# Two empty tiles of 32 bytes around the pool of the normalised activations

## Chip, core and metric

The kernel runs on one core of a Trainium2 chip. The metric is device time in microseconds (us) for one execution. The kernel before takes 1226.62 us, the median of three runs that lie between 1225.09 and 1227.04 us.

## What is computed

One decoder layer of a hybrid model on a sequence of 256 tokens, model width 2048, all in float32. The reference, cut to its frame:

```python
h = rms_norm(x, attn_norm_g[l])
proj = h @ w_in[l]                       # 2048 -> 4448 columns
shifted = token_shift(proj[..., :RWKV_SHIFT_DIM], rwkv_mu[l])
...
y_rwkv = rwkv7_mixer(h_r, h_k, h_v, h_w, h_a, h_g, ...)   # 16 heads x 64, a recurrence over tokens
y_mla = mla_mixer(c_q, c_kv, k_pe, positions, ...)        # 8 heads, causal attention
y = jnp.concatenate([y_rwkv, y_mla], axis=-1)
x = x + y @ w_out[l]
h = rms_norm(x, ffn_norm_g[l])
x = x + conv_glu_ffn(h, w_gate, w_up, conv_w, conv_b, w_down)   # 2048 -> 2 x 5632 -> 2048
return rms_norm(x, final_norm_g)
```

Some 210 MB are read from HBM, nearly all of them weights, and each weight serves only 256 tokens.

## The kernel before

**Split products.** Every large product is made of float32r matmuls. A float32 value is split in two: `hi`, its float32r rounding, and `lo`, the rest. `piece` (line 121) loads 128x1024 weights from HBM into a tile `raw`, lets ScalarE round them into `hi` (line 129) and VectorE subtract into `lo` (line 130). The activations are split in the same way, once, when they are made. Three of the four cross products are kept: hi·hi, lo·hi and hi·lo.

**Two forms of product.** In a matmul one operand is stationary (128 columns are loaded into the array) and the other is moving (it streams through).

- `prod_b` (line 153) keeps a slice of the weights stationary and streams the activations. The hi matmul (line 156) streams 512 columns, the activation's hi and its lo side by side. The lo matmul (line 159) streams 256, the activation's hi alone. One piece gives 8 hi matmuls and then 8 lo matmuls. The input projection (`in_tile`, 35 tiles of two pieces, with `x` as the activation), the up-projections of the attention (`up_b`, with `cl`) and the gate and up projections of the MLP (176 pieces, with `z`) go this way. In the profile these matmuls are called `mm<-x,hi`, `mm<-x,lo`, `mm<-z,hi` and so on.
- `prod_a` (line 169) keeps an activation slice stationary and streams 512 columns of weights, three matmuls (lines 176 to 178) for each slice: hi·hi, hi·lo, lo·hi. The output projection (with `yhi` and `ylo`) and the down projection (with `hh` and `hl`) go this way. In the profile: `mm<-hi,yhi`, `mm<-lo,hh`, `mm<-hi,hl` and so on.

**Tiles and their places.** A call of `sb.tile` with a tag draws from that tag's buffers, and each tag's buffers lie in one stretch of the on-chip memory (SBUF). A tile made with `con` (line 103) has one buffer and a name of its own. The stretches are laid out in the order in which the tags are first used in the program, each rounded up to 32 bytes, and every place is the same in all 128 partitions. The program of the kernel before, as built, has them here:

| tag (line) | buffers x bytes per partition | first byte | rest of the first byte mod 64 |
|---|---|---|---|
| reserved, and four constants of 32 | | 0 to 16,511 | |
| `a8` (line 78) | 4 x 8192 | 16,512 | 0 |
| `vec` | 1 x 1152 | 49,280 | 0 |
| `cst` | 1 x 1568 | 50,432 | 0 |
| `s4` (line 72) | 21 x 4096 | 55,584 | 32 |
| `raw` | 3 x 4096 | 141,600 | 32 |
| `hi` | 3 x 4096 | 153,888 | 32 |
| `lo` | 3 x 4096 | 166,176 | 32 |
| last tile (`rs2B`) | 1 x 1024 | 227,392 | 0 |

The last byte used is 228,415, of 229,376 that a partition has.

- `a8` (line 78) holds, one after the other, the normalised input `x` (`xs_`, line 107, made by `hl4`), the attention's `qn` and `kn`, the attention half of the output projection's activations (`yhi[1]` and `ylo[1]`, lines 805 and 806), the normalised MLP input `z` (`zs`, line 874), and at the end four pieces of weights that are split ahead of time (`wt`, line 968).
- `s4` (line 72) holds among others `cl` (the attention's latents), the other half of the output projection's activations (`yhi[0]`, `ylo[0]`), the MLP's `hh` and `hl`, and the residual `x1`.
- `raw`, `hi` and `lo` are the weight pieces.

All places inside these buffers at which a matmul's operand begins are multiples of 512 bytes from the buffer's first byte.

**Order of the work.** The order on each engine is laid out at build time by a planner that simulates the program; the first stage's loads on the SyncE queue are in an order written by hand (line 309). The stages are: input projection with the RWKV mixing between its tiles, the latents and the chunked recurrence, the attention, the output projection (first the RWKV half, `half` 0, and then the attention half, `half` 1; line 875), and then twice a block of gate and up projections followed by its down projection (24 and 20 tiles of 128 columns).

Of the kernel before, what the change touches and what calls it, by code (L numbers as in the profile page):

```python
# [17 lines left out]
P = 128  # L18
# [36 lines left out]
def hybrid_layer(ctx: ExitStack, tc: tile.TileContext, a: dict, out: bass.AP):  # L55
    nc = tc.nc
# [21 lines left out]
    def a8(n, dt=F32R):  # L78
        return sb.tile([P, 8, T], dt, tag="a8", name=nm(n), bufs=4)


    def hl4(n):
        return a8(n).rearrange("p (k s) t -> p k s t", s=2)
# [19 lines left out]
    def con(shape, n, dt=F32):  # L103
        return sb.tile(shape, dt, name=n, bufs=1)

    xT = a["xT"]
    xs_ = [hl4("x") for _ in range(4)]
    vec = con([P, NVEC], "vec")
    cst = con([P, NCST], "cst")

# [955 lines left out]
```

## Time and profile before

| what | value |
|---|---|
| median of the runs | 1226.62 us |
| the profiled execution's own time | 1224.32 us |
| its span, first to last instruction | 1222.5 us |
| matmuls on TensorE (PE) | 6993, busy 1186.5 us |
| VectorE (DVE), ScalarE (ACT), GpSimd (POOL) busy | 837.9, 599.7, 60.4 us |
| DMA | 215.82 MB, mean 177 GB/s |
| mean granted TensorE clock | 0.986 |

The profile is one execution. Its page gives the busy time of each engine, the span in 40 slices, the chain of work that ended last (followed back from the end of the program) and the costliest groups of instructions by line and operation, with their count and mean duration. The trace behind it can be asked for busy times in a stretch of the span and for the single instructions in order of time. A matmul's duration there includes its way through the array, so matmuls overlap; how fast they follow each other is read from the distance between their starts.

### The profile page before, as it was taken

The page shows a single profiled execution, that of the slowest core. Times are in us where ns is not written, and L with a number is a line of the kernel's source. Part 1 is how long each engine was busy: PE and PEld are TensorE (multiplying, and loading weights), DVE is VectorE, ACT ScalarE, POOL GpSimd, SP SyncE. Part 2 cuts the span into 40 slices and gives each one's busy share as a digit, 9 for nine tenths or more (in the row PEclk, how much of TensorE's full clock was granted, in tenths as well). Part 3 has the DMA queues.
Part 4 walks back from the last instruction along what each step waited for, and adds up shares of the span by engine and source line. Part 5 has one row for each costly group of instructions (what it writes and reads, how often), then busy time and mean ns, then how long its engine had stood idle before and what let it go on. Part 6 is the DMA issues. An engine that isn't in the chain of part 4 may idle for free.

```text
span 1222.5 us, 18434 instructions
## 1 busy us (share of the span) xinstructions
PE 1186.5 (97%) x6993; PEld 1001.6 (82%) x6993; DVE 837.9 (69%) x1359; ACT 599.7 (49%) x939; POOL 60.4 (5%) x202
## 2 busy tenths in 40 slices
PE   7989979999989999999999999999999999999996
PEld 5878868888847888888888888888888888888885
DVE  6898659868985656777777676454577777766563
ACT  6684425635334455555555554333455555554442
POOL 3400100002120001000000000000000000000000
PEclk9989999999999999999999999999999999999998
DMA  8735544744513555655555555666655555566662
GB/s 298 207 116 157 145 147 135 204 141 143 166 64 104 177 174 172 201 188 181 186 187 190 189 185 179 195 190 194 203 182 188 189 186 185 183 223 205 208 209 85
DMA packets 71017, 215.82 MB, mean 177 GB/s; under 512 B 17616, under 2 KB 17872, under 8 KB 70928
## 3 DMA queue, kind: packets, MB, share of 16 engines
q1 hardware_dynamic: 69776, 211.84, 53.9%
q10 hardware_dynamic: 768, 2.05, 0.6%
q8 instruction: 55, 0.90, 0.3%
q0 software_dynamic: 384, 0.75, 0.2%
q14 instruction: 34, 0.28, 0.1%
HBM read 210.48 MB, written 3.41 MB: 175 GB/s over the span
## 4 chain that ended last, share of the span: by engine, by line
PE 90%; DVE 3%; DMA 2%; ACT 2%; issue 1%; POOL 1%; SPq 0%; ACTq 0%; DVEq 0%; POOLq 0%
PE mm L156 38%; PE mm L159 19%; PE mm L177 9%; PE mm L178 9%; PE mm L176 9%; PE pg L514 1%; DMA raw<-in_win 1%; DVE lo L130 1%; ACT hi L129 1%; PE px L658 1%; DMA rp<-in_pos 0%; DMA Lp<-dL 0%; PE psc L834 0%; PE py L658 0%; PE psc L832 0%
## 5 line engine op out<-in xcount | busy, mean ns | idle before, releaser
L130 DVE TENSOR_TENSOR lo<-raw,hi 128x1024 fp32r<-128x1024 f32 x376 | 460.5, 1225 | 294.1 <-ACT hi L129 288.1
L129 ACT CAST hi<-raw 128x1024 fp32r<-128x1024 f32 x376 | 395.1, 1051 | 478.7 <-issue 259.7
L156 PE MATMUL mm<-z,hi 128*128 128x512 f32 x1408 | 356.9, 395 | 0.0
L156 PEld LDWEIGHTS mm<-z,hi 128*128 128x128 f32 x1408 | 253.3, 188 | 48.8
L159 PEld LDWEIGHTS mm<-z,lo 128*128 128x128 f32 x1408 | 192.8, 188 | 15.4
L159 PE MATMUL mm<-z,lo 128*128 128x256 f32 x1408 | 197.7, 282 | 0.0
L156 PE MATMUL mm<-x,hi 128*128 128x512 f32 x528 | 147.2, 415 | 15.7 <-DVE rp L249 8.2
L177 PE MATMUL mm<-lo,hh 128*128 128x512 f32 x336 | 130.7, 389 | 0.0
L178 PE MATMUL mm<-hi,hl 128*128 128x512 f32 x336 | 130.7, 389 | 0.0
L156 PEld LDWEIGHTS mm<-x,hi 128*128 128x128 f32 x528 | 98.7, 198 | 35.6 <-ACT hi L129 8.2
L176 PE MATMUL mm<-hi,hh 128*128 128x512 f32 x336 | 119.7, 389 | 0.0
L159 PEld LDWEIGHTS mm<-x,lo 128*128 128x128 f32 x528 | 75.3, 192 | 8.8 <-DVE lo L130 1.5
L159 PE MATMUL mm<-x,lo 128*128 128x256 f32 x528 | 81.3, 290 | 0.7 <-DVE lo L130 0.7
L176 PEld LDWEIGHTS mm<-hi,hh 128*128 128x128 f32 x336 | 63.1, 188 | 13.1
L177 PEld LDWEIGHTS mm<-lo,hh 128*128 128x128 f32 x336 | 63.1, 188 | 13.0
L178 PEld LDWEIGHTS mm<-hi,hl 128*128 128x128 f32 x336 | 63.1, 188 | 13.0
L177 PE MATMUL mm<-lo,yhi 128*128 128x512 f32 x128 | 51.4, 402 | 0.0
L178 PE MATMUL mm<-hi,ylo 128*128 128x512 f32 x128 | 50.6, 396 | 0.0
L176 PE MATMUL mm<-hi,yhi 128*128 128x512 f32 x128 | 49.1, 398 | 0.0
L940 POOL MEMSET gt<- 128x2 f32 x44 | 4.3, 99 | 587.2 <-DVE hl L952 570.0
L177 PEld LDWEIGHTS mm<-lo,yhi 128*128 128x128 f32 x128 | 24.1, 188 | 6.1 <-DVE lo L130 0.6
L176 PEld LDWEIGHTS mm<-hi,yhi 128*128 128x128 f32 x128 | 24.2, 189 | 5.2
(287 smaller groups left out, 1126.4 us busy)
## 6 DMA issues: line engine op xcount, KB each, us to landing
raw<-in_wgu SPq DMA_DIRECT2D x176, 512.0 KB, 3.3
raw<-in_wdn SPq DMA_DIRECT2D x88, 512.0 KB, 4.2
raw<-in_win SPq DMA_DIRECT2D x70, 512.0 KB, 3.7
raw<-in_wout SPq DMA_DIRECT2D x32, 512.0 KB, 3.5
raw<-in_wuq SPq DMA_DIRECT2D x6, 512.0 KB, 3.3
xraw<-in_xT SPq DMA_DIRECT2D x4, 512.0 KB, 6.1
xt<-in_x SPq DMA_DIRECT2D x4, 512.0 KB, 6.5
raw<-in_wuk SPq DMA_DIRECT2D x4, 512.0 KB, 3.3
```

Source lines behind the costliest of these rows:

```text
L129: S.copy(hi, raw)
L130: last_lo[0] = V.tensor_tensor(lo, raw, hi.bitcast(F32), ALU.subtract).ins
L156: PE.matmul(acc, hi[:, j * P:(j + 1) * P], act(kt0 + j), start=first and j == 0, stop=False, skip_group_check=True)
L159: PE.matmul(acc[:, :T], lo[:, j * P:(j + 1) * P], act(kt0 + j)[:, 0, :], start=False, stop=last and j == n - 1, skip_group_check=True)
L176: PE.matmul(accs[tb], ah, wh, start=first and j == 0, stop=False)
L177: PE.matmul(accs[tb], ah, wl, start=False, stop=False)
L178: PE.matmul(accs[tb], al, wh, start=False, stop=last and j == n - 1)
L514: PE.matmul(pg[h][:, o:o + P], BK[pp][hs, gg, w * 2 + r, :, :], AR[pp][hs, gg, w * 2 + r, :, :], start=o == 0, stop=True, skip_group_check ...
L658: PE.matmul(dst[HS[h], a_ * 64:(a_ + 1) * 64], lhsT, rhs, start=n == 0 and a_ == 0, stop=True, skip_group_check=True)
L940: nc.gpsimd.memset(gt[:, 0:2], 0.0)
```

## The change

Two tiles are made, each of 8 float32 values (32 bytes) per partition, and each is set to zero once by GpSimd. Nothing reads them. The first stands ahead of the first use of `a8`, the second behind it and ahead of `vec`:

```diff
     def con(shape, n, dt=F32):
         return sb.tile(shape, dt, name=n, bufs=1)
 
+    pad = con([P, 8], "pad")
+    nc.gpsimd.memset(pad, 0.0)
     xT = a["xT"]
     xs_ = [hl4("x") for _ in range(4)]
+    pad2 = con([P, 8], "pad2")
+    nc.gpsimd.memset(pad2, 0.0)
     vec = con([P, NVEC], "vec")
     cst = con([P, NCST], "cst")
```

By the rule of the layout above, `a8` begins 32 bytes later, and everything behind it 64 bytes later.

## The prediction

> **What bounds the kernel now.** First the page: its busy shares and the chain of work that ended last.
>
> ```profile
> PE 1186.5 (97%) x6993; PEld 1001.6 (82%) x6993; DVE 837.9 (69%) x1359; ACT 599.7 (49%) x939; POOL 60.4 (5%) x202
> PE 90%; DVE 3%; DMA 2%; ACT 2%; issue 1%; POOL 1%; SPq 0%; ACTq 0%; DVEq 0%; POOLq 0%
> ```
>
> TensorE is busy 97% of the span and 90% of the chain. A busy engine can still be slower than it need be, so the question is what one matmul costs at each place.
>
> Then the busy times by stage: input projection (75:176 and 182:273), and the two blocks of gate and up (474:746, 877:1102).
>
> ```profile
> 75.00:176.00 101.00, 101.00 (x644) 87.18 (x643) 76.68 (x155) 47.87 (x78) 6.08 (x20) 1.00 0.46 136
> 182.00:273.00 91.00, 88.82 (x773) 77.56 (x774) 75.68 (x154) 45.35 (x78) 3.27 (x19) 0.95 0.54 158
> 474.00:746.00 272.00, 272.00 (x1543) 237.00 (x1542) 196.15 (x298) 144.95 (x226) 7.17 (x40) 1.00 0.56 186
> 877.00:1102.00 225.00, 225.00 (x1273) 195.90 (x1272) 159.49 (x237) 116.10 (x177) 1.69 (x17) 1.00 0.57 190
> ```
>
> The columns are the stretch, its length, and the busy time of PE, weight loads, DVE, ACT and POOL, then the granted clock, the DMA share and GB/s. In all but one PE is never idle at full clock, while DVE is at 72% of the first gate-and-up block (196.15 of 272) and DMA at 56%. There, a nanosecond off a matmul is a nanosecond off the span.
>
> Last the timeline of PE's matmuls, where the distance between starts is what one costs. Gate and up, three pieces; then the down projection, first and last of 18 rows:
>
> ```profile
> 709.98 2.03 PE L156 MATMUL mm<-z,hi 128*128 128x512 f32 x8
> 711.84 1.12 PE L159 MATMUL mm<-z,lo 128*128 128x256 f32 x8
> 712.80 2.03 PE L156 MATMUL mm<-z,hi 128*128 128x512 f32 x8
> ...
> 718.46 0.86 PE L156 MATMUL mm<-z,hi 128*128 128x512 f32 x3
> ```
>
> ```profile
> 780.06 0.39 PE L176 MATMUL mm<-hi,hh 128*128 128x512 f32 x1
> ...
> 783.91 0.39 PE L178 MATMUL mm<-hi,hl 128*128 128x512 f32 x1
> ```
>
> A piece of gate and up takes 8.48/3 = 2.827 us. Its eight hi matmuls take 1.86/8 = 0.2325 us each, its lo matmuls 0.96/8 = 0.120. In the down projection 17 steps take 3.85 us: 0.2265 each, for the same 512 columns. `z` lies in `a8`, which begins at a multiple of 64 bytes; `hi`, `hh` and `hl` all begin 32 bytes past one. So the slow matmul mixes two remainders, and the fast one doesn't. Two more places test that. The output projection changes its activation from `s4` to `a8` between its halves, with all else the same (15 matmuls between the first two rows, 18 between the last two; the second half begins at 426.71). And the last pieces, `wt`, are weights that lie in `a8`, with `hh` from `s4` (36 matmuls):
>
> ```profile
> 420.33 0.39 PE L176 MATMUL mm<-hi,yhi 128*128 128x512 f32 x1
> ...
> 423.73 0.85 PE L176 MATMUL mm<-hi,yhi 128*128 128x512 f32 x3
> ...
> 426.71 0.39 PE L177 MATMUL mm<-lo,yhi 128*128 128x512 f32 x1
> ...
> 430.93 0.39 PE L177 MATMUL mm<-lo,yhi 128*128 128x512 f32 x1
> ```
>
> ```profile
> 1203.49 0.39 PE L176 MATMUL mm<-wt,hh 128*128 128x512 f32 x1
> ...
> 1211.89 0.39 PE L176 MATMUL mm<-wt,hh 128*128 128x512 f32 x1
> ```
>
> In half 0: 3.40/15 = 0.2267. In half 1: 4.22/18 = 0.2344. With `wt` moving: 8.40/36 = 0.2333, although the other engines have little left to do there. Whether the operand in `a8` moves (`z`, `wt`) or is stationary (`yhi` in half 1), the matmul is some 7 ns slower. I read this as a cost of mixed remainders, about 0.0066 us for each 512-column matmul.
>
> **The change part by part.** *Places.* `pad` takes 16,512 and `a8` moves to 16,544 = 258 x 64 + 32. `pad2` follows, so `vec` moves by 64, to 49,344, and all behind it by 64: remainders mod 64 stay. The last byte moves from 228,415 to 228,479, within 229,376. After that `a8` has the remainder of `s4`, `hi` and `lo`, and no float32r product mixes any more.
>
> *A gate-and-up piece.* If all its hi matmuls go at 0.2267 and the lo ones stay at 0.120, it takes 8 x 0.2267 + 8 x 0.120 = 2.774 us: 0.053 less. This is the upper bound, as the fast pace is not reached at once. After an interruption the matched half 0 needs nine matmuls to settle, and `cl`, matched too and in the same `prod_b` form, changes from hi to lo after four:
>
> ```profile
> 395.45 0.39 PE L176 MATMUL mm<-hi,yhi 128*128 128x512 f32 x1
> ...
> 397.53 0.39 PE L176 MATMUL mm<-hi,yhi 128*128 128x512 f32 x1
> ...
> 400.03 0.39 PE L178 MATMUL mm<-hi,ylo 128*128 128x512 f32 x1
> ```
>
> ```profile
> 307.04 1.09 PE L156 MATMUL mm<-cl,hi 128*128 128x512 f32 x4
> ...
> 308.44 1.09 PE L156 MATMUL mm<-cl,hi 128*128 128x512 f32 x4
> ```
>
> The nine take 2.08/9 = 0.2311 each, the eleven after them 2.50/11 = 0.2273. So settling costs up to 9 x 0.0044 = 0.040 us. If each piece pays it whole, it takes 2.814 and saves only 0.013: the lower bound. `cl` needs 1.40 us for four hi and four lo, 0.013 over 4 x 0.2267 + 4 x 0.120 = 1.387: the price of a change of form. `cl` is the nearest row (same form, matched). A piece of `z` changes form once, which leaves 0.053 - 0.013 = 0.040; priced as two units of `cl`, 2 x 1.40 = 2.80, it saves 0.027. I take 0.034, between the two.
>
> *Sum.* Gate and up: 88 tiles x 2 = 176 pieces x 0.034 = 6.0 us. Input projection: the hi matmuls in the two stretches in which PE is filled are counted by the busy times of line 156 alone,
>
> ```profile
> 75.00:176.00 101.00, 58.49 (x217) 38.21 (x216) 1.00 0.46 136
> 182.00:273.00 91.00, 56.41 (x208) 38.97 (x208) 0.95 0.54 158
> ```
>
> 425/8 = 53 pieces x 0.034 = 1.8. The idle stretch between the two waits for a chain of work that PE's own tiles start, so it moves ahead with them. The pieces before 75 us I cost at nothing: the chain there runs through the weights' DMA and the rotary tables, which hide them; if that cover is thin, 17 pieces bring 0.6 more. Output projection, half 1: 4 x 4 x 12 = 192 matmuls x 0.0077 = 1.5, less eight interruptions by transposes at up to 0.040: 1.2. `wt`: 4 x 12 = 48 x 0.0066 = 0.3. In sum 9.3.
>
> *The memsets.* Both stand at the head of POOL, ahead of `ones` and of the load of the positions, with which the chain begins:
>
> ```profile
> 0.24 0.10 POOL L1056 MEMSET const-float32-0.0<- 128x1 f32 x1 [0.24 <-issue]
> 0.28 0.10 POOL L1056 MEMSET const-float32-1.0<- 128x1 f32 x1
> 0.73 0.20 POOL L294 MEMSET ones<- 128x128 f32 x1 [0.29 <-POOLq L1056]
> 1.28 0.76 POOL L241 DMA_DIRECT2D rp<-in_pos  x1 [0.35 <-issue]
> ```
>
> Small memsets follow each other in 0.04 us and last 0.10, so two delay this load, and behind it the first matmuls, by 0.08 to 0.2. I take 0.1. Nothing else waits: no instruction reads the pads.
>
> So 9.3 - 0.1 = 9.2 us: span 1222.5 - 9.2 = 1213.3, own time of the profiled execution 1224.32 - 9.2 = 1215.1. That execution was 2.3 us under the median, so the median comes to 1226.62 - 9.2 = **1217.4 us**. By the lower bound: 229 x 0.013 + 1.2 + 0.3 = 4.5, 1222.1; by the upper: 229 x 0.053 + 1.5 + 0.3 = 13.9, 1212.7. What is late next is still PE: a piece of 2.79 us leaves DVE (72% of 2.827) a quarter idle.
>
> **The rivals.**
>
> *The 64-byte remainder is not what counts.* `a8` and the `hi` buffers differ by 137,376 bytes, 160 more than a multiple of 256. After the change it is 137,408, still 192 more than one. If the cost hangs on a coarser unit, such as 128 or 256 bytes, or on `a8` lying far away, the operands stay unmatched: no change, 1226.7. For it: within `s4`, `hi` and `lo` all places agree to 512 bytes, so no row separates 64 from 128. Against it: the step from 0.2267 to 0.2333 is the time of 0.0066/0.2267 x 512 = 15 columns, some 60 bytes of float32 in a partition, an estimate that points to a unit of 64. Chance 0.16. The Trainium skill ("SBUF — State Buffer", "Specifications (TRN2)" and "Who interferes with whom") speaks for this rival: it has lines of 16 bytes, and two independent read ports for TensorE, one for each operand. By that rule neither 32 bytes nor the pairing would matter, and the trace disagrees with it in the jump at 426.71.
>
> *The new distance is a worse one.* If what counts is the distance of the two operands in a coarser unit, 32 bytes more can also move them to the worst place. One further step of 0.0066 for 229 x 8 + 192 + 48 = 2072 matmuls is +13.7 us: 1240.3. It decides as soon as the hi matmuls of `z` start over 0.2344 apart. Against it: no row has such a pace. Chance 0.07.
>
> *The order or the clock shifts.* The planner sees two more instructions and may place others differently; and the clock gate shows a halved clock after idle stretches:
>
> ```profile
> 70.00:77.00 7.00, 7.00 (x27) 5.37 (x25) 6.36 (x18) 6.23 (x16) 0.10 (x1) 0.63 0.19 68
> ```
>
> One more such stretch (0.37 of 7 us lost) costs 2.6 us; with no gain from the places 1229.2. Chance 0.05. One fewer gives the same amount on the other side.
>
> *The gain is absorbed.* PE gets ahead and waits for pieces, since ACT and DVE take theirs in a fixed order: half of 9 us is left at worst, 1222. Against it: the shares above. Chance 0.04.
>
> **How the numbers follow.** The forecast has 0.68, with 1212 to 1222.5 as its own range. Faster (over 0.2%, 2.5 us, about what a measurement of this kernel can tell from no change): 0.68, 0.03 of the absorbed gain and 0.01 of the shifted order, 0.72. Same: 0.16 and 0.01 of the absorbed gain, 0.17. Slower: 0.07 and 0.04, 0.11. The range of 1211.5 to 1228 holds the forecast, the unchanged time and the absorbed gain, 0.86 with some of the tails lost; only the worse distance and an added slow stretch lie beyond it.
>
> **What would show it.** In the profile after: hi matmuls of `z` 0.227 to 0.231 apart and a piece of 2.77 to 2.81 us; half 1 of the output projection at the pace of half 0; `wt` at 0.227; the down projection unchanged at 0.2265. If `z` stays at 0.2325, the remainder isn't the cause. If `wt` and half 1 get faster and `z` doesn't, the change of form from hi to lo eats the gain, and some 2 us are left.

## The result, and the profile after

| | before | after |
|---|---|---|
| median of four runs each, side by side | 1226.83 us | 1209.95 us |
| lowest and highest | 1225.09, 1228.63 | 1207.96, 1211.42 |
| ratio, 95% interval | | 0.9872, 0.9853 to 0.989 |
| profiled execution, own time | 1224.32 us | 1211.42 us |
| its span | 1222.5 us | 1209.5 us |

The change makes the kernel 16.9 us faster. The forecast was 9.2 us, and the median lies 1.55 us below the range. The profiled execution of after happens to be the longest of its four, 1.5 us over their median, and that of before lies 2.5 us under its own, so the traces show 13.0 us of span and not 16.9.

Page of after, busy shares and chain of waits:

```profile
PE 1172.9 (97%) x6993; PEld 996.0 (82%) x6993; DVE 837.2 (69%) x1359; ACT 599.3 (50%) x939; POOL 59.4 (5%) x204
PE 88%; DVE 5%; DMA 2%; ACT 2%; issue 2%; POOL 1%; SPq 0%; ACTq 0%; DVEq 0%; POOLq 0%
```

The number of matmuls is the same, and PE is busy 13.6 us less (1186.5 - 1172.9), while the other engines' sums hardly move. As built, the order of instructions on PE, DVE, ACT and SP is the same in both kernels, and POOL has the two memsets more: nothing was rearranged. So matmuls became cheaper, and the costliest groups of the page say which. First before, then after (busy us, mean ns of one):

```profile
L156 PE MATMUL mm<-z,hi 128*128 128x512 f32 x1408 | 356.9, 395 | 0.0
L159 PE MATMUL mm<-z,lo 128*128 128x256 f32 x1408 | 197.7, 282 | 0.0
```

```profile
L160 PE MATMUL mm<-z,hi 128*128 128x512 f32 x1408 | 351.3, 392 | 0.0
L163 PE MATMUL mm<-z,lo 128*128 128x256 f32 x1408 | 191.6, 278 | 0.0
```

The hi matmuls of gate and up give 5.6 us, and the lo matmuls, which the prediction left at their old price, give 6.1. The timeline of PE in after shows the same in single pieces:

```profile
703.64 2.00 PE L160 MATMUL mm<-z,hi 128*128 128x512 f32 x8
705.47 1.07 PE L163 MATMUL mm<-z,lo 128*128 128x256 f32 x8
706.38 1.99 PE L160 MATMUL mm<-z,hi 128*128 128x512 f32 x8
708.21 1.11 PE L163 MATMUL mm<-z,lo 128*128 128x256 f32 x8
709.15 2.00 PE L160 MATMUL mm<-z,hi 128*128 128x512 f32 x8
```

Two pieces take 5.51 us, 2.755 each, against 2.827. Eight hi take 1.83 (0.229 each, where 0.2267 was expected once settled). Eight lo take 0.91 and 0.94 in turn (0.1138 and 0.1175, where 0.120 was expected).

The stages, each from its first weight load to that of the next, worked out from both traces:

| stage | before, us | after, us | change |
|---|---|---|---|
| input projection | 273.34 | 271.90 | -1.44 |
| latents and attention up-projections | 45.20 | 45.16 | -0.04 |
| attention | 35.50 | 36.94 | +1.44 |
| output projection, half 0 and half 1 | 72.21 + 47.55 | 71.79 + 47.38 | -0.42 - 0.17 |
| gate and up, both blocks | 272.80 + 226.25 | 266.18 + 220.70 | -12.17 |
| down, both blocks | 130.47 + 97.83 | 130.47 + 97.84 | +0.01 |
| `wt`, and the tail | 10.97 + 10.37 | 10.78 + 10.38 | -0.18 |

Of 13.0 us, 12.2 are in gate and up, 0.069 us for each of 176 pieces. PE stays the bound there: the first block of after, busy times by stretch,

```profile
473.17:739.35 266.18, 266.18 (x1550) 234.66 (x1549) 196.66 (x298) 145.44 (x227) 7.08 (x40) 1.00 0.56 190
```

has PE busy without a gap, DVE at 74% (196.66 of 266.18). The input projection is the least sure row. Three kernels below repeat it: e1 and e10 have the distances of after, e2 those of before. In the profiled executions the stage takes 273.34 and 274.86 us (before, e2) against 271.90, 270.61 and 270.94 (after, e1, e10), some 3 us less on the mean, so the 1.44 of this one pair is on the low side.

In this pair the gain of the input projection is given back in the attention. There the clock tells why; first before, then after, the column behind POOL's is the granted clock:

```profile
341.00:349.00 8.00, 7.35 (x32) 3.42 (x32) 7.47 (x10) 3.18 (x7) 0.00 (x0) 0.79 0.00 1
```

```profile
341.00:349.00 8.00, 8.00 (x17) 3.01 (x16) 6.29 (x9) 3.73 (x8) 0.00 (x0) 0.57 0.00 1
```

A stretch at half clock that begins near 341 us lasted 3.41 us in the one execution and 6.83 in the other. All such stretches of a span, without the one at the program's end, add up to 27.3 us before and 30.7 after. Across the fourteen profiled executions of this study the sum goes from 23.9 to 44.4 us, so this is a difference between executions. No run shows that the places change it. The granted clock of after's four executions has a mean of 0.986; but e1, which has the same distances, has 0.9835 over four, no more than the 0.9834 of the thirteen executions of before measured beside it, and is still 15.4 us faster than they are.

### The profile page after: what moved, and what is told of

It reads as the page before. It is cut to its first block, busy times and chain, and to the rows that moved or that the text cites. A ratio compares the mean times of both kernels' runs of the same rounds, so it can differ in the third digit from the quotient of the medians.

```text
span 1209.5 us, 18436 instructions
## 1 busy us (share of the span) xinstructions
PE 1172.9 (97%) x6993; PEld 996.0 (82%) x6993; DVE 837.2 (69%) x1359; ACT 599.3 (50%) x939; POOL 59.4 (5%) x204
## 3 DMA queue, kind: packets, MB, share of 16 engines
q10 hardware_dynamic: 768, 2.05, 0.5%
HBM read 210.48 MB, written 3.41 MB: 177 GB/s over the span
## 4 chain that ended last, share of the span: by engine, by line
PE 88%; DVE 5%; DMA 2%; ACT 2%; issue 2%; POOL 1%; SPq 0%; ACTq 0%; DVEq 0%; POOLq 0%
PE mm L160 37%; PE mm L163 18%; PE mm L181 9%; PE mm L180 9%; PE mm L182 9%; DVE lo L134 1%; PE pg L518 1%; DMA raw<-in_win 1%; ACT hi L133 1%; DMA xt<-in_x 0%; DMA rp<-in_pos 0%; DMA Lp<-dL 0%; PE psc L838 0%; POOL rt L213 0%; PE psc L836 0%
## 5 line engine op out<-in xcount | busy, mean ns | idle before, releaser
L160 PE MATMUL mm<-z,hi 128*128 128x512 f32 x1408 | 351.3, 392 | 0.0
L163 PEld LDWEIGHTS mm<-z,lo 128*128 128x128 f32 x1408 | 188.3, 188 | 14.4
L163 PE MATMUL mm<-z,lo 128*128 128x256 f32 x1408 | 191.6, 278 | 0.0
L160 PE MATMUL mm<-x,hi 128*128 128x512 f32 x528 | 144.7, 411 | 17.2 <-DVE h L169 8.8
L182 PEld LDWEIGHTS mm<-hi,ylo 128*128 128x128 f32 x128 | 24.2, 189 | 5.3 <-issue 0.3
```

The costliest lines, as they stand in the source:

```text
L160: PE.matmul(acc, hi[:, j * P:(j + 1) * P], act(kt0 + j), start=first and j == 0, stop=False, skip_group_check=True)
L163: PE.matmul(acc[:, :T], lo[:, j * P:(j + 1) * P], act(kt0 + j)[:, 0, :], start=False, stop=last and j == n - 1, skip_group_check=True)
L182: PE.matmul(accs[tb], al, wh, start=False, stop=last and j == n - 1)
```

## Experiments

The prediction's theory: a float32r matmul is slow where the two operands begin at different remainders mod 64. Its rivals: the absolute place of `a8`, or the distance of the operands in a coarser unit. All experiments change places alone. Call *d* the first byte of the moving operand less that of the stationary one, mod 256. For `z` or `x` over `hi`, *d* is 96 before (16,512 - 153,888 = -537 x 256 + 96) and 64 after. It is the same over `lo`, which lies 48 x 256 bytes behind `hi`, and for `wt` over `hh`. In half 1 the weights move and `a8` is stationary, so *d* is 256 less that: 160 and 192.

### Each tile alone

`e1_behind_only` leaves `pad` out and gives `pad2` 32 bytes; `e2_ahead_only` leaves `pad2` out.

```diff
-    pad = con([P, 8], "pad")
-    nc.gpsimd.memset(pad, 0.0)
```

```diff
-    pad2 = con([P, 8], "pad2")
-    nc.gpsimd.memset(pad2, 0.0)
```

> Only the second empty tile (32 bytes, behind a8): a8 stays at 16,512 (remainder 0 mod 64), everything behind it moves by 32 to remainder 0. The distance between a8 and the weight tiles is the same as in the changed kernel, but no operand has remainder 32. Theory 'pairing' (equal remainders of the two operands, or their distance, set the pace): as the changed kernel, a gate-and-up piece of 2.767 us and about 1210 us. Theory 'own place' (a moving operand in a8 is fast at remainder 32): as before, 2.827 us and about 1227. If weights at remainder 0 are bad or good by themselves, the down projection leaves 0.2267 us for each matmul.

> Only the first empty tile (32 bytes, ahead of a8): a8 and everything behind it move by 32, so all distances are those of the kernel before; a8 has remainder 32 mod 64, the weights 0. Theory 'pairing': as before, a piece of 2.827 us and about 1227 us. Theory 'own place': as the changed kernel, 2.767 us and about 1210.

Measured: e1 1210.75 us, ratio 0.9882 (0.9865 to 0.9898); e2 1226.72, ratio 1.0007 (0.9997 to 1.0017). In e2 a piece takes as long as before; timeline of PE:

```profile
706.85 2.03 PE L158 MATMUL mm<-z,hi 128*128 128x512 f32 x8
...
709.68 2.03 PE L158 MATMUL mm<-z,hi 128*128 128x512 f32 x8
```

In e2 every large operand is 32 bytes further on, so all distances are those of before: 2.83 us for a piece. In e1 `a8` stays at its old place, 0 mod 64, and the rest moves by 32: the distances are those of after, and the stages of gate and up are the same to 0.01 us (266.18 and 220.70). So a common shift of all operands by 32 bytes, either way, changes nothing, and the distance between them is the cause. The first tile does nothing by itself. The second would do the whole work with the first left out.

### Other distances

`pad2` alone with 64, 128, 160, 192 and 224 bytes (`e3` and `e5` to `e8`), and 32 bytes ahead with 96 behind (`e4_ahead_32_behind_96`). For example `e3_behind_64` against e1, and e4 against after:

```diff
-    pad2 = con([P, 8], "pad2")
+    pad2 = con([P, 16], "pad2")
```

```diff
-    pad2 = con([P, 8], "pad2")
+    pad2 = con([P, 24], "pad2")
```

> One empty tile of 64 bytes behind a8: the distance grows by 64 against the kernel before, the remainders mod 64 are those of before (0 and 32, mixed). Theory 'remainder mod 64': as before, a piece of 2.827 us, about 1227 us. Theory 'distance in a unit of 128 bytes or more': another pace than both kernels, since the distance is 224 past a multiple of 256 (before 160, changed 192); by steps of 0.0066 us for each 512-column matmul, 2.72 to 2.88 us a piece.

> Empty tiles of 32 bytes ahead of a8 and 96 behind: a8 as in the changed kernel, the distance to the weight tiles a multiple of 256 bytes. Theory 'remainder mod 64': as the changed kernel, a piece of 2.767 us and the second half of the output projection at 0.2333 us for each matmul, about 1210 us. Theory 'distance in a coarser unit': as the down projection, whose operands lie whole multiples of 512 apart: the second half of the output projection falls to 0.2267 us, and a piece to 2.74 to 2.79 us; 1205 to 1212.

> One empty tile of 128 bytes behind a8. Take m for the place of the moving operand less that of the stationary one, in bytes modulo 256: for z over hi it was 96 before, 64 in the changed kernel, 32 and 0 with 64 and with 32 + 96 bytes; for the second half of the output projection, where the roles are swapped, 160, 192, 224 and 0. Here z has 224 and that half 32. Theory 'unit of 128': the same as the kernel before, since 128 bytes are no change: a piece of 2.827 us, 1226 us. Theory 'unit of 256': another pace; by the second half of the output projection at m = 224, z's hi matmuls at 0.2331 us, so a piece of 2.80 to 2.84.

> One empty tile of 160 bytes behind a8: z has m = 192, the second half of the output projection 64. Theory 'unit of 128': as the changed kernel, a piece of 2.767 us and that half at 0.2331 us for each matmul, 1210 us. Theory 'unit of 256': the two change places: that half falls to 0.2292 us (as wt at m = 64), and z's hi matmuls go at 0.2331 (as that half did at 192), a piece of 2.80 us or more, 1217 us or more.

> One empty tile of 192 bytes behind a8: z has m = 160, the second half of the output projection 96. Theory 'unit of 128': as with 64 bytes behind, a piece of 2.809 us, 1220 us. Theory 'unit of 256': z's hi matmuls as that half before (m = 160), 0.2333 us, and that half as z before (m = 96), 0.2333; a piece of 2.80 to 2.84.

> One empty tile of 224 bytes behind a8: m = 128 for both. Theory 'unit of 128': as with 32 + 96 bytes, the second half of the output projection at 0.2267 us, a piece of 2.793 us, 1218 us. Theory 'unit of 256': no row for it yet; that half away from 0.2267, a piece of 2.75 to 2.84 us.

Mean steps from one matmul's start to the next, in ns, over the whole trace; for half 1 the pace inside a run of matmuls, with *d* in brackets (for e4 once it has settled; 228.0 with the settling). The times are medians, each with its ratio to the executions of before that were measured beside it; e6 rests on two executions:

| kernel | *d* of `z` | `z` hi | `z` lo | half 1 | `wt` | us | ratio, 95% |
|---|---|---|---|---|---|---|---|
| e4 | 0 | 230.0 | 119.1 | 226.7 (0) | 226.7 | 1218.84 | 0.9937, 0.9922 to 0.9952 |
| e3 | 32 | 233.4 | 117.5 | 233.1 (224) | 233.4 | 1220.20 | 0.9952, 0.9937 to 0.9966 |
| after, e1 | 64 | 229.0 | 115.7 | 233.1 (192) | 229.2 | 1209.95 | 0.9872, 0.9853 to 0.989 |
| before, e2 | 96 | 233.0 | 120.3 | 234.1 (160) | 233.6 | 1226.83 | |
| e8 | 128 | 232.7 | 118.6 | 232.8 (128) | 233.2 | 1220.90 | 0.9960, 0.9944 to 0.9975 |
| e7 | 160 | 233.8 | 118.1 | 233.5 (96) | 234.2 | 1224.31 | 0.9984, 0.997 to 0.9997 |
| e6 | 192 | 232.7 | 114.0 | 229.1 (64) | 233.3 | 1216.09 | 0.9917, 0.9888 to 0.9945 |
| e5 | 224 | 232.7 | 118.9 | 233.1 (32) | 233.3 | 1222.22 | 0.9982, 0.9957 to 1.0007 |

e3 already breaks the unit of 64: its *d* differs from before by 64, so the remainders mod 64 are mixed as before, and yet a piece is shorter. Timeline of e3:

```profile
704.78 2.03 PE L158 MATMUL mm<-z,hi 128*128 128x512 f32 x8
706.65 1.10 PE L161 MATMUL mm<-z,lo 128*128 128x256 f32 x8
707.58 2.03 PE L158 MATMUL mm<-z,hi 128*128 128x512 f32 x8
```

Hi is slow as ever (1.87/8 = 0.234), lo is faster (0.93/8 = 0.116). So hi and lo each have a dependence of their own. The pair of *d* = 64 and 192 shows that 128 isn't the unit either; in e6 the two forms of product change sides:

```profile
706.42 2.02 PE L158 MATMUL mm<-z,hi 128*128 128x512 f32 x8
708.28 1.07 PE L161 MATMUL mm<-z,lo 128*128 128x256 f32 x8
709.19 2.02 PE L158 MATMUL mm<-z,hi 128*128 128x512 f32 x8
...
428.82 0.39 PE L178 MATMUL mm<-hi,yhi 128*128 128x512 f32 x1
...
433.40 0.39 PE L180 MATMUL mm<-hi,ylo 128*128 128x512 f32 x1
```

`z` hi is slow with 1.86/8 = 0.2325, and half 1, whose *d* is now 64, takes 4.58/20 = 0.229, the very pace that `z` hi and `wt` have in after. In after half 1 was still slow, 4.66/20 = 0.233:

```profile
426.24 0.40 PE L181 MATMUL mm<-lo,yhi 128*128 128x512 f32 x1
...
430.90 0.40 PE L180 MATMUL mm<-hi,yhi 128*128 128x512 f32 x1
```

For a 512-column matmul the table holds in both directions: 226.7 ns at *d* = 0 once settled, 229 at 64, and 233 to 234 at 32, 96, 128, 160, 192 and 224, whichever of the two operands lies in `a8`.

e4 is the kernel that the prediction described: *d* is 0, and nothing mixes. Timeline of e4:

```profile
702.04 2.00 PE L160 MATMUL mm<-z,hi 128*128 128x512 f32 x8
703.88 1.12 PE L163 MATMUL mm<-z,lo 128*128 128x256 f32 x8
704.84 2.00 PE L160 MATMUL mm<-z,hi 128*128 128x512 f32 x8
...
428.27 0.39 PE L181 MATMUL mm<-lo,yhi 128*128 128x512 f32 x1
...
433.26 0.39 PE L182 MATMUL mm<-hi,ylo 128*128 128x512 f32 x1
```

A piece takes 2.80 us, the lo matmuls 0.96/8 = 0.120, and half 1 4.99/22 = 0.2268. Against before, its gate and up lose 3.25 + 2.70 = 5.95 us, half 1 loses 1.10 and `wt` 0.32. Yet e4's median is 8.9 us above that of after. 6.2 of it are in gate and up: 1408 x 3.4 ns for the lo matmuls (119.1 against 115.7), and 1408 x 1.0 for the hi ones. Those reach 226.7 only with the last three of the eight in a piece and average 230.0. Of the rest, the input projection of the profiled executions has 2.05 (273.95 against 271.90), half 1 and `wt` take 1.1 back, and 1.8 is which executions were profiled.

### The period, and a finer step

`e10_period_256` moves all that lies behind `a8` by 256 bytes more than after; `e12_a8_16_on` moves the operands in `a8` by 16 bytes inside their buffers.

```diff
-    pad2 = con([P, 8], "pad2")
+    pad2 = con([P, 72], "pad2")
```

```diff
-        return sb.tile([P, 8, T], dt, tag="a8", name=nm(n), bufs=4)
+        t = sb.tile([P, 8 * T + 64], dt, tag="a8", name=nm(n), bufs=4)
+        return t[:, 4:4 + 8 * T].rearrange("p (k t) -> p k t", t=T)
```

(In e12 `rsB` and `rs2B` share a buffer, to make room.)

> The changed kernel with 288 in place of 32 bytes behind a8: 256 bytes more distance, all else equal. Theory 'unit of 256': all paces as in the changed kernel, a piece of 2.767 us, z's hi 0.2290, lo 0.1157, 1210 us. Theory 'a larger unit' (512 or more): another pace; before, m = 96 modulo 256 gave 2.827.

> The changed kernel with every operand in a8 16 bytes further on (each buffer 256 bytes longer and used from its 16th byte, and rs2B put in the place of rsB to make room): z over hi at m = 80 in place of 64, between the paces at 64 (a piece of 2.767 us) and at 96 (2.827). Theory 'steps of 32 bytes or coarser count': one of the two, 2.767 or 2.827. Theory 'each 16 bytes count': a pace of its own. About 1210 to 1228.

e10: 1209.89 us, ratio 0.9871 (0.9851 to 0.9891), the same steps and the same 266.18 and 220.70 us of gate and up as after. With e6 beside it, which is 128 bytes from after and differs, 256 bytes more change nothing at this distance, and 128 do. e10 rests on two executions. e12: 1218.59, ratio 0.994 (0.9915 to 0.9965). Timeline of e12:

```profile
706.52 2.01 PE L161 MATMUL mm<-z,hi 128*128 128x512 f32 x8
708.37 1.11 PE L164 MATMUL mm<-z,lo 128*128 128x256 f32 x8
709.32 2.01 PE L161 MATMUL mm<-z,hi 128*128 128x512 f32 x8
```

Here *d* is 80: hi 1.85/8 = 0.231, lo 0.95/8 = 0.119, a piece 2.80. So 16 bytes matter, and half of after's gain is gone; gate and up take 494.36 us, against 486.88 in after and 499.05 before.

### A better combination?

By the table, the best lo (114.0 at 192) doesn't go with the best hi. If each matmul had the price of its own *d*, a tile between `hi` and `lo` would join them. `e9_lo_apart_128` puts 128 bytes there, on after (hi 64, lo 192); `e11_hi_0_lo_192` has hi at 0 by a `pad2` of 96 bytes and lo at 192 by a gap of 64.

```diff
+    gap = []
+
     def piece(src, dst=None):
...
             hi = sb.tile([P, 1024], F32R, tag="hi", name=nm("hi"), bufs=NHI)
+            if not gap:
+                gap.append(con([P, 32], "pad3"))
+                nc.gpsimd.memset(gap[0], 0.0)
             lo = sb.tile([P, 1024], F32R, tag="lo", name=nm("lo"), bufs=NLO)
```

> The changed kernel with one more empty tile of 128 bytes between the weights' hi and lo tiles: z over hi stays at m = 64, z over lo goes from 64 to 192 (m: place of the moving less that of the stationary operand, modulo 256). Theory 'each matmul by the m of its own two operands': z's hi matmuls stay at 0.2290 us, its lo matmuls fall from 0.1157 to 0.1140, a piece about 2.75; in the down projection the one matmul in three that streams lo goes from 0.2267 to 0.2327, 2.1 us more; 1207 to 1211. Theory 'only the tiles' common distance counts': no change of the lo matmuls, 1210 to 1212.

> Empty tiles of 32 bytes ahead of a8, 96 behind it, and 64 between hi and lo: z over hi at m = 0, z over lo at m = 192. Theory 'each matmul by its own m': hi 0.2267 once settled, lo 0.1140, a piece between 2.725 and 2.76 with the change of form, the down projection's lo matmuls (m = 64) at 0.229, 0.9 us more; 1205 to 1211. Theory 'the two forms disturb each other': the hi matmuls don't settle, 2.77 or more, 1211 or more.

e9: 1213.86 us (1208.42 to 1215.84), ratio 0.9896 (0.987 to 0.9922); e11: 1221.41, ratio 0.9965 (0.9951 to 0.9979). Timeline of e9, gate and up and then the down projection:

```profile
707.50 2.00 PE L165 MATMUL mm<-z,hi 128*128 128x512 f32 x8
709.33 1.07 PE L168 MATMUL mm<-z,lo 128*128 128x256 f32 x8
710.25 2.00 PE L165 MATMUL mm<-z,hi 128*128 128x512 f32 x8
...
800.26 0.39 PE L185 MATMUL mm<-hi,hh 128*128 128x512 f32 x1
800.48 0.40 PE L186 MATMUL mm<-lo,hh 128*128 128x512 f32 x1
800.72 0.39 PE L187 MATMUL mm<-hi,hl 128*128 128x512 f32 x1
```

A piece takes 2.75, and lo has its 114 ns as hoped: gate and up lose 1.57 us more than in after (485.31 against 486.88). But `lo` lies at another distance from `hh` now, and that product takes 0.24 in these rows where its neighbours take 0.22 (233.9 ns over the whole trace, against 226.9 and 226.2): the down projections grow by 1.31 + 0.99 = 2.30 us (131.78 and 98.83). The stages show this better than the times: the profiled execution of e9, 1208.42 us, is the fastest of four and has the least time at half clock of all fourteen, while its median lies 5.4 us above it. Timeline of e11:

```profile
707.19 2.00 PE L165 MATMUL mm<-z,hi 128*128 128x512 f32 x8
709.03 1.11 PE L168 MATMUL mm<-z,lo 128*128 128x256 f32 x8
709.97 2.00 PE L165 MATMUL mm<-z,hi 128*128 128x512 f32 x8
...
800.04 0.39 PE L186 MATMUL mm<-lo,hh 128*128 128x512 f32 x1
...
802.83 0.39 PE L186 MATMUL mm<-lo,hh 128*128 128x512 f32 x1
```

Here lo takes 0.94/8 = 0.1175 at *d* = 192, not 0.114. In the down projection all three products are slow, 2.79/12 = 0.2325, though two of them still have *d* = 0. e4 differs from e11 by the gap alone and keeps the down projections at 130.48 and 97.84 us, where e11 has 133.63 and 100.20; the gap moves `lo` and what lies behind it, and so an operand of the third product alone. That contradicts a price of each matmul by itself. What stands next to it seems to count too, but no run separates this further. No version here is clearly faster than the changed kernel.

## Why the prediction was wrong

**Right.** PE was the bound, the pace of a float32r matmul hangs on where its two operands lie, and the down projection kept its pace. Timeline of after, down projection and `wt`:

```profile
778.70 0.39 PE L182 MATMUL mm<-hi,hl 128*128 128x512 f32 x1
...
783.91 0.39 PE L181 MATMUL mm<-lo,hh 128*128 128x512 f32 x1
...
1188.58 0.40 PE L180 MATMUL mm<-wt,hh 128*128 128x512 f32 x1
...
1198.90 0.40 PE L180 MATMUL mm<-wt,hh 128*128 128x512 f32 x1
```

With 23 matmuls between its rows the down projection goes at 5.21/23 = 0.2265. The memsets cost no more than was said; timeline of POOL in after:

```profile
0.73 0.10 POOL L107 MEMSET pad<- 128x8 f32 x1 [0.29 <-POOLq L1060]
0.77 0.10 POOL L111 MEMSET pad<- 128x8 f32 x1
...
1.34 0.77 POOL L245 DMA_DIRECT2D rp<-in_pos  x1 [0.33 <-issue]
```

The load of the positions is issued 0.06 us later (1.34 against 1.28), inside the 0.1 us priced.

**The step that failed** is "after that `a8` has the remainder of `s4`, `hi` and `lo`, and no float32r product mixes any more". The remainder mod 64 isn't the unit: the distance mod 256 counts, and 16 bytes of it already do (e12). The 15 columns that the prediction turned into some 60 bytes were no measure of the unit. After the change *d* is 64, not 0, and e4 shows what that sentence would have brought: 5.95 us in gate and up (forecast 6.0), 1.10 in half 1 (1.2), 0.32 in `wt` (0.3), and 1218.84 us in all (1217.4). So the working belongs to a kernel that the change doesn't make, and even there the close agreement is in part luck. Of e4's 5.95 us the hi matmuls give 1408 x 3.0 ns = 4.2, and the lo ones, priced at nothing, 1408 x 1.2 = 1.7. The input projection, forecast to gain 1.8, takes 273.95 us in e4's trace, no less than before.

**The term that fell with it** is "the lo ones stay at 0.120". The mean lo went from 120.3 to 115.7 ns: 1408 x 4.6 = 6.5 us that the sum didn't have. Hi went from 233.0 to 229.0: 1408 x 4.0 = 5.6. Together 12.1, the 12.17 us of the stages. The upper bound, 0.053 for a piece, counted hi alone; the piece gained 0.069. One row of before spoke of another price for lo. Between the two `cl` rows that the prediction shows stand the four lo matmuls of `cl`, with *d* = 0; timeline of before:

```profile
307.97 0.64 PE L159 MATMUL mm<-cl,lo 128*128 128x256 f32 x4
308.44 1.09 PE L156 MATMUL mm<-cl,hi 128*128 128x512 f32 x4
```

They take 0.47/4 = 0.1175 us each, where those of `z` took 0.120. An estimate from this one row puts 1408 x 0.0025 = 3.5 us more into the upper bound, 1209.2 us in place of 1212.7.

**Other points.** Half 1, forecast at the pace of half 0, only went from 0.2341 to 0.2331, since its *d* is 192: its 1.2 us became 0.17. `wt` came to 10.32/45 = 0.2293 instead of 0.227. These two are the signs, set beforehand, that told the unit apart; a gain in gate and up alone would not have. The input projection gained 1.44 in this pair and some 3 over the five executions (forecast 1.8). The rival of a coarser unit was right about the unit, 256 bytes, and wrong in taking the new distance for as bad as the old; the rival of a worse distance had the sign wrong. The new distance gives the shortest piece among the eight multiples of 32, and that is luck, since it was chosen for another reason.

**Open.** The runs show which distances are fast, not why, nor why neighbours count as in e11. Except where `lo` stands apart (e9, e11), the stationary operand of the next matmul lies at the same distance mod 256 as the matmul's own, so these runs don't show which of the two counts. Steps below 16 bytes were not tried, nor other lengths of matmul, nor a separate place for every operand.

## What to carry to other kernels

Where matmuls fill the span and one form has different paces at different places, compare the distance of the two operands mod 256 bytes before looking for waits: here one unused tile of 32 bytes (e1) is worth 1.2%. A unit read off two places in a trace is a guess, since two points fit 64, 128 and 256 alike; a ladder of eight pads settles it, and it has to be measured for each form of matmul that uses the buffers. Each move shifts every product that shares a buffer, so count the products that are fast already.

## What was not expected of the hardware

- A 512-column float32r matmul takes 226.7 to 234 ns, and a 256-column one 114.0 to 120.3 ns, by the operands' distance mod 256, with the neighbours of e11 as the exception seen; the fastest distance of the one (0) is among the slow ones of the other (119.1 at 0).
- 16 bytes more take `z` hi from 229.0 to 231.2 ns and lo from 115.7 to 118.8 (e12).
- A matmul whose own distance is unchanged can slow down by its neighbours: with e11's gap, which among the operands of the down projection moves only `lo`, all three of its products go from 0.2265 to 0.2325.
- Stretches at half clock differ widely between profiled executions, from 23.9 to 44.4 us in sum without the one at the end. The execution with 44.4, of e8, has a span of 1227.8 us, while the median of e8's runs is 1220.9. One profile against another can mislead by several us here; the down projection, whose distances are the same in twelve of the fourteen, repeats to 0.06.
